# Eight buffers of split weights at eight byte offsets modulo 128 in a hybrid recurrent block in float32

## The chip, the cores and the metric

One Trainium2 chip, one of its cores. The metric is the time of one execution on the device in microseconds. The engines are named as in the profile: PE is TensorE's matmul, PEld its weight load (the load of the operand that stands still), DVE is VectorE, ACT ScalarE, POOL GpSimd, SP SyncE, whose queue issues nearly all transfers.

## The reference

One layer over 512 positions of width 1024, in float32: a mixer of two recurrent branches (HGRN2 and mLSTM, four heads of 128 each), a cross attention to 256 memory rows, and a feed-forward part with a causal convolution of three taps. Each ends in a residual and a layer norm:

```python
mix = hybrid_mixer(x, w_in[l], b_in[l], lower_bounds[l], hg_norm_w[l],
                   ml_conv_w[l], ml_conv_b[l], ml_norm_w[l], w_out[l])
x = layer_norm(ALPHA * x + mix, ln1_g[l], ln1_b[l])
ca = memory_cross_attention(x, mem, ca_wq[l], ca_wkv[l], ca_wo[l])
x = layer_norm(ALPHA * x + ca, ln2_g[l], ln2_b[l])
ff = conv_ffn(x, ffn_w_up[l], ffn_conv_w[l], ffn_conv_b[l], ffn_w_down[l])
x = layer_norm(ALPHA * x + ff, ln3_g[l], ln3_b[l])
```

The work is in the dense products with `w_in` (1024 x 4104), `w_out`, `ca_wq`, `ca_wkv`, `ca_wo` (1024 wide), `ffn_w_up` (1024 x 5632) and `ffn_w_down` (2816 x 1024).

## The kernel before

**Products in three terms.** Each operand of a dense product is held as a rounded high part (float32r) and a low part, the rest. `mm3` (line 155) issues three matmuls for one product: high by high (L156), high by low (L157), low by high (L158). The activations are split once where they are made (`split_evict`, line 244) into tiles such as `xTh` and `xTl`. The weights are split on the way: a transfer brings up to 8 KiB a partition into `raw` (three buffers), and `split` (line 119) makes two units of it. For each unit ACT copies 1024 elements a partition into a buffer `wh`, rounding them (L125), and DVE subtracts that from `raw` into a buffer `wl` (L126). There are four `wh` and four `wl` of 4096 bytes a partition, used in turn; a copy into one waits until the matmuls that read its earlier contents are done.

**Two kinds of stage.** In `slab` (line 160) the activations stand still in the array and 512 columns of weights stream past: for each unit of two k-blocks, over up to four blocks of 128 positions, high, low and high parts of the weights are streamed in turn. The slabs are four column ranges of `w_in` (HI by a loop written out at lines 278 to 303, HG, MV, MO), `w_out`, the values of the cross attention, `ca_wo` and `ffn_w_down`. In `col_tile` (line 200) the weights stand still, 128 columns at a time, and the activations stream: `w_in`'s other ranges, the keys (256 columns), `ca_wq` and `ffn_w_up` (halves of 256 columns at its beginning). In the profile's names `mm<-wh,xTh` is a matmul that streams `wh` while `xTh` stands still, and `mm<-x2h,wh` one that streams `x2h` past `wh`. One unit feeds 24 matmuls of 512 columns in either kind, fewer where there are only two blocks.

**The gate columns.** The 8 columns of `w_in` for the mLSTM gates take a turn of the four `wh` buffers by themselves (line 350): POOL clears the buffer, ACT and DVE write high and low parts into it, and the matmuls of L362 and L363 load it.

**Where tiles lie.** The pools follow one another within a partition: `const`, `wp` (`raw`, `wh`, `wl`, the gate columns), `xp` (ten activation tiles of 8 KiB), `sm` (small vectors), and then `q1` or `q2`. Paddings (`CONST_PAD`, `WP_PAD`, `SM_PAD`) make `raw`, `wh`, `wl` and every large activation tile begin at a multiple of 128 bytes; slices of them begin at further multiples of 512 bytes.

**Order.** The order of the opening (transposes of x and the HI product) is written out by hand; elsewhere each engine runs its instructions in the order of the program as it was scheduled. Nothing of that order is named in the change.

Of the kernel before, what the change touches and what calls it, by code (L numbers as in the profile page):

```python
# [10 lines left out]
F32R = mybir.dt.float32r  # L11
# [6 lines left out]
P = 128  # L18
# [3 lines left out]
KT = D // P  # L22
# [7 lines left out]
QSCALE = P ** -0.5  # L30
CSCALE = 256 ** -0.5
WARM = 7
CONST_PAD, WP_PAD, SM_PAD = 40, 64, 16
HQ, HF, HI, HG, MQ, MK, MV, MO, MI, MF = (0, 512, 1024, 1536, 2048, 2560, 3072, 3584, 4096, 4100)


# [1 line left out]
def hybrid_block_kernel(  # L38
# [31 lines left out]
    wp = ctx.enter_context(tc.tile_pool(name="wp", bufs=1))  # L70
# [26 lines left out]
    def f32(t):  # L97
        return t.bitcast(F32)
# [12 lines left out]
    def load_raw(src_list, shape):  # L111
# [4 lines left out]
            nc.sync.dma_start(dst, src)  # L116
        return rv

    def split(src, shape):
        h = wp.tile([P, 1024], F32R, name="wh", tag="wh", bufs=4)  # L120
        l = wp.tile([P, 1024], F32R, name="wl", tag="wl", bufs=4)
        a, c = shape
        hv = h.rearrange("p (a c) -> p a c", a=a)
        lv = l.rearrange("p (a c) -> p a c", a=a)
        A.copy(hv, src)  # L125
        V.tensor_sub(lv, src, f32(hv))  # L126
        return hv, lv

    def slab_units(w, c0, nk, raw=None):

        k, per = 0, (2 if raw is not None else 4)
        while k < nk:
            n = min(4, nk - k)
            if k or raw is None:
                raw = load_raw(
                    lambda rv, k=k, n=n: [(rv[:, j:min(j + per, n), :],
                                           w[(k + j) * P:(k + min(j + per, n)) * P, c0:c0 + 512]
                                           .rearrange("(k p) c -> p k c", p=P)) for j in range(0, n, per)],
                    (4, 512))
            for u in range(0, n, 2):  # L140
                h, l = split(raw[:, u:u + 2, :], (2, 512))
                yield k + u, 2, h, l
            k += n

    def col_units(w, c0, n):

        for j in range(0, n, 2):
            raw = load_raw(
                lambda rv, j=j: [(rv, w[:, c0 + j * P:c0 + (j + 2) * P]
                                  .rearrange("(k p) c -> p k c", p=P))], (8, 256))  # L150
            for i in range(2):
                h, l = split(raw[:, :, i * P:(i + 1) * P], (8, P))
                yield j + i, h, l
# [193 lines left out]

    wif = wp.tile([P, KT, 8], F32, name="wif")
    nc.sync.dma_start(wif, w_in0[:, MI:MI + 8].rearrange("(k p) c -> p k c", p=P))
    wifh = wp.tile([P, 1024], F32R, name="wh", tag="wh", bufs=4).rearrange("p (k c) -> p k c", k=KT)  # L350
    G.memset(f32(wifh), 0.0)
    for j in range(2):
        src = wif[:, :, 4 * j:4 * j + 4]
        o, o2 = slice(32 * j, 32 * j + 4), slice(64 + 32 * j, 68 + 32 * j)
# [183 lines left out]
    for hd in range(4):  # L538
        o = hgrn_head(hd)
# [36 lines left out]
    for j in range(4):  # L576
        ps = mm_bank()
        for i in range(2):
            for b in range(2):
                k = 2 * j + i  # L580
# [257 lines left out]
    def up_units(i):  # L838
        raw = load_raw(lambda rv: [(rv[:, :, j * P:(j + 1) * P],
                                    ffn_w_up[0][:, j * DFF + i * P:j * DFF + (i + 1) * P]  # L840
                                    .rearrange("(k p) c -> p k c", p=P)) for j in range(2)], (8, 256))
        return [split(raw[:, :, j * P:(j + 1) * P], (8, P)) for j in range(2)]
# [4 lines left out]
    for half in range(2):  # L847
        c0 = half * 256
        for i in range(early):
            for j in range(2):  # L850
                if (half, i, j) == (0, 1, 1):
                    x2_last()
                h, l = units[i][j]
# [31 lines left out]
def build(shapes):  # L885
    import concourse.bacc as _bacc

    nc = _bacc.Bacc("TRN2", target_bir_lowering=False, num_devices=1, dynamic_dma_scratch_size=1024)
    args = [nc.dram_tensor(f"in_{n}_dram", shapes[n], F32, kind="ExternalInput").ap() for n in _INS]
    args.append(nc.dram_tensor("out_0_dram", (1, S, D), F32, kind="ExternalOutput").ap())  # L890
    with tile.TileContext(nc) as tc:
        hybrid_block_kernel(tc, *args)
    return nc
# [9 lines left out]
```

## Time and profile before

| | |
|---|---|
| three runs | 828.69, 829.31, 829.79 us; median 829.31 |
| profiled execution | 829.24 us, of which the span is 827.5 |
| PE busy | 809.6 us (98%), 4051 matmuls |
| PEld busy | 682.2 us (82%), beside PE |
| DVE busy | 504.4 us (61%) |
| ACT busy | 323.1 us (39%) |
| POOL busy | 31.6 us (4%) |
| transfers | 87.88 MB, 106 GB/s over the span |

The span runs from the first to the last instruction. A matmul's recorded duration overlaps that of the next, so a busy PE does not tell how fast it goes: the distance from one start to the next does, and it is worked out from the rows of a timeline. "Idle before" is the time for which an engine did nothing ahead of an instruction, with what ended it.

### The profile page before, as it was taken

The numbers are of one execution on the slowest core, as the hardware profiler recorded it, in microseconds if no ns is written. First come the engines' busy times: TensorE is split into PE (matmuls) and PEld (weight loads), VectorE is DVE, ScalarE is ACT, GpSimd is POOL, SyncE is SP. The second block draws the span as 40 slices with busy tenths as digits, with TensorE's granted clock in tenths as the row PEclk, the third lists the DMA queues.
The fourth block names the chain that finished last, engine by engine and source line by source line (L and its number), as shares of the span: only waits on it lengthen the run. The fifth ranks groups of instructions, "written<-read, shape, count | busy, mean of one in ns | idle before, by whom it ended". The sixth has DMA issues, their size and how long they took to land.

```text
span 827.5 us, 10149 instructions
## 1 busy us (share of the span) xinstructions
PE 809.6 (98%) x4051; PEld 682.2 (82%) x4051; DVE 504.4 (61%) x863; ACT 323.1 (39%) x443; POOL 31.6 (4%) x52
## 2 busy tenths in 40 slices
PE   8979999999999999999999999999999999999996
PEld 7868877778779888889988988888888888888885
DVE  4374378888878289338638685566665666224237
ACT  4169653344235215226512364444444444221110
POOL 1000100010120000000001000000000000000001
PEclk9999999999999999999999999999999999999998
DMA  7845534034426613431311533333333322242102
GB/s 250 188 93 134 133 65 102 12 91 102 143 74 220 239 51 137 168 102 52 102 51 51 154 104 101 102 102 102 102 103 101 91 83 83 75 153 70 59 0 102
DMA packets 85156, 87.88 MB, mean 106 GB/s; under 512 B 3184, under 2 KB 64880, under 8 KB 85108
## 3 DMA queue, kind: packets, MB, share of 16 engines
q1 hardware_dynamic: 84524, 84.58, 34.4%
q10 hardware_dynamic: 584, 2.64, 0.8%
q8 instruction: 32, 0.52, 0.3%
q14 instruction: 16, 0.13, 0.0%
HBM read 85.10 MB, written 2.12 MB: 105 GB/s over the span
## 4 chain that ended last, share of the span: by engine, by line
PE 88%; DVE 5%; DMA 3%; POOL 1%; ACT 1%; issue 1%; SPq 0%; DVEq 0%; ACTq 0%; POOLq 0%
PE mm L156 27%; PE mm L157 27%; PE mm L158 27%; DMA raw<-in_w_in_dram 3%; PE mx L254 1%; PE mx L605 1%; PE mx L617 1%; POOL ss L451 1%; DMA xin<-in_x_dram 1%; PE mx L492 1%; PE mx L493 1%; PE mx L156 0%; PE mx L158 0%; PE mx L157 0%; PE mx L445 0%
## 5 line engine op out<-in xcount | busy, mean ns | idle before, releaser
L126 DVE TENSOR_TENSOR wl<-raw,wh 128x1024 fp32r<-128x1024 f32 x138 | 168.1, 1223 | 233.1 <-ACT wh L125 232.1
L125 ACT CAST wh<-raw 128x1024 fp32r<-128x1024 f32 x138 | 145.2, 1055 | 247.9 <-PE mm L158 135.1
L156 PE MATMUL mm<-x2h,wh 128*128 128x512 f32 (+1 forms) x384 | 142.8, 372 | 0.0
L157 PE MATMUL mm<-x2l,wh 128*128 128x512 f32 (+1 forms) x384 | 142.6, 371 | 0.0
L158 PE MATMUL mm<-x2h,wl 128*128 128x512 f32 (+1 forms) x384 | 142.6, 371 | 0.0
L158 PEld LDWEIGHTS mm<-x2h,wl 128*128 128x128 f32 x384 | 72.4, 188 | 12.6
L157 PEld LDWEIGHTS mm<-x2l,wh 128*128 128x128 f32 x384 | 72.4, 188 | 12.5
L156 PEld LDWEIGHTS mm<-x2h,wh 128*128 128x128 f32 x384 | 72.4, 188 | 12.3
L157 PE MATMUL mm<-wl,hTh 128*128 128x512 f32 (+1 forms) x198 | 72.4, 366 | 0.0
L156 PE MATMUL mm<-wh,hTh 128*128 128x512 f32 (+1 forms) x198 | 72.4, 366 | 0.0
L826 DVE SCALAR_TENSOR_TENSOR fc<-mm,cols,fc 128x511 f32<-128x511 f32 x88 | 65.7, 747 | 1.5
L158 PE MATMUL mm<-wh,hTl 128*128 128x512 f32 (+1 forms) x180 | 65.8, 365 | 0.0
L156 PE MATMUL mm<-wh,xTh 128*128 128x512 f32 x128 | 52.1, 407 | 0.0
L158 PE MATMUL mm<-wh,xTl 128*128 128x512 f32 x128 | 51.6, 403 | 0.0
L157 PE MATMUL mm<-wl,xTh 128*128 128x512 f32 x128 | 51.4, 401 | 0.0
L156 PE MATMUL mm<-xTh,wh 128*128 128x512 f32 x128 | 51.2, 400 | 0.0
L157 PE MATMUL mm<-xTl,wh 128*128 128x512 f32 x128 | 51.0, 399 | 0.0
L158 PE MATMUL mm<-xTh,wl 128*128 128x512 f32 x128 | 50.9, 397 | 0.0
L156 PEld LDWEIGHTS mm<-wh,hTh 128*128 128x128 f32 x198 | 37.4, 189 | 6.1
L157 PEld LDWEIGHTS mm<-wl,hTh 128*128 128x128 f32 x198 | 37.4, 189 | 6.1
L158 PEld LDWEIGHTS mm<-wh,hTl 128*128 128x128 f32 x180 | 33.9, 189 | 5.5
L835 ACT CAST hTh<-fc 128x512 fp32r<-128x512 f32 x22 | 13.7, 622 | 55.8 <-DVE fc L834 55.8
(274 smaller groups left out, 1401.3 us busy)
## 6 DMA issues: line engine op xcount, KB each, us to landing
raw<-in_ffn_w_up_dram SPq DMA_DIRECT2D x44, 512.0 KB, 4.3
raw<-in_w_in_dram SPq DMA_DIRECT2D x14, 1024.0 KB, 8.1
raw<-in_ffn_w_down_dram SPq DMA_DIRECT2D x10, 1024.0 KB, 5.0
raw<-in_ca_wkv_dram SPq DMA_DIRECT2D x8, 1024.0 KB
raw<-in_w_out_dram SPq DMA_DIRECT2D x4, 1024.0 KB, 10.1
raw<-in_ca_wq_dram SPq DMA_DIRECT2D x4, 1024.0 KB, 7.2
raw<-in_ca_wo_dram SPq DMA_DIRECT2D x4, 1024.0 KB
wt<-scr ACTq DMA_DIRECT2D x4, 640.0 KB
```

The lines of the kernel that those rows point to most:

```text
L125: A.copy(hv, src)
L126: V.tensor_sub(lv, src, f32(hv))
L156: T.matmul(ps, ah, bh, start=first, stop=False, skip_group_check=True)
L157: T.matmul(ps, ah, bl, start=False, stop=False, skip_group_check=True)
L158: T.matmul(ps, al, bh, start=False, stop=last, skip_group_check=True)
L254: T.transpose(ps[:, i * P:(i + 1) * P], src[:, k * P:(k + 1) * P], ident)
L451: G.tensor_tensor(out_, out_, neghalf[:, 0:n], op=OP.pow)
L492: T.matmul(at[:, s], ke[:, s], qe[:, s], start=True, stop=True, skip_group_check=True)
L493: T.matmul(at[0:CH, b * P + CH:(b + 1) * P], kxe[:, b, :], qbo[:, b, :], start=True, stop=True, skip_group_check=True)
L605: T.matmul(ps[:, 0:LEN[j]], kT_[:, j * P:(j + 1) * P], qT_[:, j * P:], start=True, stop=True)
L826: V.scalar_tensor_tensor(y[:, s:], ps[:, :S - s], col(FCW + (2 - s) * 44 + ft), y[:, s:], op0=OP.mult, op1=OP.add)
L835: A.copy(kslice(hTh, i), g)
```

## The change

Each of the eight buffers becomes a tile of its own, 1056 elements long instead of 1024, and the 1024 that are used begin at an offset within it: 16, 32, 48 and 8 bytes for the four high parts, 80, 96, 112 and 64 bytes for the four low parts. The tiles themselves are a multiple of 128 bytes long and begin at one, so these are the offsets modulo 128 to the activations. `split_tiles` hands out a high and a low part by turns. The gate columns take a pair and use its high part. `WP_PAD` goes from 64 to 32 elements.

```diff
-CONST_PAD, WP_PAD, SM_PAD = 40, 64, 16
+CONST_PAD, WP_PAD, SM_PAD = 40, 32, 16
+
+PHASES = {"wh": (16, 32, 48, 8), "wl": (80, 96, 112, 64)}
...
+    turn = [0]
+
+    def split_tiles():
+
+        i = turn[0] % 4
+        turn[0] += 1
+        out = []
+        for t in ("wh", "wl"):
+            o = PHASES[t][i] // 4
+            out.append(wp.tile([P, 1056], F32R, name=t, tag=f"{t}{i}")[:, o:o + 1024])
+        return out
+
     def split(src, shape):
-        h = wp.tile([P, 1024], F32R, name="wh", tag="wh", bufs=4)
-        l = wp.tile([P, 1024], F32R, name="wl", tag="wl", bufs=4)
+        h, l = split_tiles()
...
-    wifh = wp.tile([P, 1024], F32R, name="wh", tag="wh", bufs=4).rearrange("p (k c) -> p k c", k=KT)
+    wifh = split_tiles()[0].rearrange("p (k c) -> p k c", k=KT)
```

## Rows read from the trace of the kernel before

**Rows 1.** Stretches: length; busy us (instructions) of PE, PEld, DVE, ACT, POOL; clock; transfers.

```profile
30.00:70.00 40.00, 35.65 (x155) 29.06 (x154) 24.90 (x50) 23.44 (x27) 0.00 (x0) 0.96 0.48 118
...
480.00:760.00 280.00, 280.00 (x1245) 232.23 (x1244) 156.54 (x188) 110.14 (x138) 0.00 (x0) 1.00 0.33 100
```

**Rows 2.** Waits of PE, whole span: us in total, times, longest.

```profile
PE mx L404 <- ACT ae L399: 4.3, 1, 4.3
PE mx L445 <- DVE y L534: 2.4, 3, 1.1
PE mx L254 <- DMA xin<-in_x_dram: 1.6, 1, 1.6
...
PE mx L617 <- DVE den L627: 0.3, 1, 0.3
```

**Rows 3.** Timeline of PE in the FFN, weights standing: start, us, instruction.

```profile
545.73 0.39 PE L156 MATMUL mm<-x2h,wh 128*128 128x512 f32 x1
...
551.85 0.39 PE L156 MATMUL mm<-x2h,wh 128*128 128x512 f32 x1
```

**Rows 4.** Timeline of PE in the first slab, weights streaming.

```profile
20.17 0.39 PE L158 MATMUL mm<-wh,xTl 128*128 128x512 f32 x1
...
35.13 0.39 PE L158 MATMUL mm<-wh,xTl 128*128 128x512 f32 x1
```

**Rows 5.** Timeline of PE at the end of the last slab, 256 columns.

```profile
816.87 0.28 PE L156 MATMUL mm<-wh,hTh 128*128 128x256 f32 x1
...
819.99 0.28 PE L158 MATMUL mm<-wh,hTh 128*128 128x256 f32 x1
```

**Rows 6.** The whole span as a stretch, instructions with a `wh`, then with a `wl`.

```profile
0.00:827.50 827.50, 666.07 (x2268) 416.48 (x2268) 168.45 (x140) 145.58 (x140) 0.95 (x1) 1.00 0.36 106
...
0.00:827.50 827.50, 423.13 (x1126) 213.23 (x1126) 168.13 (x138) 1.00 0.36 106
```

**Rows 7.** A stretch at the lower clock, and PE's timeline in it.

```profile
61.90:65.10 3.20, 3.20 (x8) 2.52 (x9) 1.28 (x3) 3.19 (x5) 0.00 (x0) 0.50 0.00 0
...
62.41 0.63 PE L157 MATMUL mm<-xTl,wh 128*128 128x512 f32 x1
...
64.54 0.63 PE L156 MATMUL mm<-xTh,wh 128*128 128x512 f32 x1
```

**Rows 8.** Timeline of PE where 512 columns follow 256 in the FFN.

```profile
481.79 0.40 PE L156 MATMUL mm<-x2h,wh 128*128 128x512 f32 x1
...
482.95 0.39 PE L158 MATMUL mm<-x2h,wl 128*128 128x512 f32 x1
...
483.85 0.39 PE L156 MATMUL mm<-x2h,wh 128*128 128x512 f32 x1
```

**Rows 9.** Groups of PEld by form: count, busy us, mean ns, idle before.

```profile
L156 PEld LDWEIGHTS mm<-x2h,wh 128*128 128x128 f32 x384 | 72.4, 188 | 12.3
...
L493 PEld LDWEIGHTS mx<-xo 128*64 128x64 f32 x32 | 3.1, 134 | 2.1 <-issue 0.2
```

**Rows 10.** Groups of DVE and of ACT by form, same columns.

```profile
L126 DVE TENSOR_TENSOR wl<-raw,wh 128x1024 fp32r<-128x1024 f32 x138 | 168.1, 1223 | 233.1 <-ACT wh L125 232.1 <-PE mm L581 0.8
...
L826 DVE SCALAR_TENSOR_TENSOR fc<-mm,cols,fc 128x511 f32<-128x511 f32 x44 | 32.8, 744 | 0.0
...
L704 DVE SCALAR_TENSOR_TENSOR xres<-xres,lnrs,lnb 128x512 f32<-128x512 f32 x24 | 16.9, 746 | 0.0
...
L125 ACT CAST wh<-raw 128x1024 fp32r<-128x1024 f32 x138 | 145.2, 1055 | 247.9 <-PE mm L158 135.1 <-PE mm L157 79.3 <-DMA raw<-in_w_in_dram 13.4
```

**Rows 11.** Waits of ACT, then of DVE, between 500 and 760 us.

```profile
ACT wh L125 <- PE mm L158: 40.0, 10, 4.4
...
DVE wl L126 <- ACT wh L125: 104.0, 48, 4.3
```

**Rows 12.** The chain that ended last, in order of time: start, us, what.

```profile
18.76 20.91 DMA raw<-in_w_in_dram
39.77 1.06 ACT wh L125
```

## The prediction

> **What bounds the kernel now.** I read the stretches of the span first, then what ended TensorE's idle time, then TensorE's rows one by one. The stretches [rows 1] show TensorE busy in nearly every microsecond: 280.00 of 280.00 us between 480 and 760 us, and short of full only for moments, such as 4.35 us between 30 and 70 us. The waits [rows 2] show six groups in which TensorE idled: 4.3 us for ScalarE, 2.4 us for VectorE, 1.6 us for a transfer, and three smaller ones, the last of 0.3 us. None waits for a split weight buffer. So the time is the number of matmuls times the distance from one start to the next. A busy TensorE does not say how good that distance is, so I worked it out from starts: in the FFN 27 matmuls from 545.73 to 551.85 us, more than the 24 that one pair of buffers feeds, take 6.12 us, 226.7 ns each [rows 3]. In a slab, where the weights stream and the activations stand still, 66 matmuls from 20.17 to 35.13 us take 14.96 us, again 226.7 ns [rows 4]. Matmuls of 256 columns start every 3.12 us / 26 = 120.0 ns [rows 5]. The 256 columns between the two sizes cost 106.7 ns, 0.417 ns a column (the 2.4 GHz level, granted 1.00 in those stretches). So 512 columns stream in 213.3 ns, and each matmul of either size carries 13.3 ns on top.
>
> The split buffers are operands of 2268 + 1126 = 3394 matmuls [rows 6]. 3394 x 13.3 ns = 45.2 us of the span is this surplus. The change can pay, or cost, almost only there.
>
> **What is known of the surplus.** At the 1.2 GHz level (granted 0.50 from 61.90 to 65.10 us) five starts from 62.41 to 64.54 us are 426 ns apart: 512 columns at 0.833 ns are 426.7, and no surplus is left [rows 7]. It is no fixed cost in ns of a matmul; it shows where the stream runs at its full rate. It is also 32 columns of 4 bytes at 0.417 ns, so just as long as 128 bytes of one partition's stream, the very period in which the change places its buffers. But 128 weights of 4 bytes being loaded beside it could give 32 of something too. And it is not quite constant: where matmuls of 512 columns follow those of 256, the first five take 482.95 - 481.79 = 1.16 us instead of 1.133, and from then on the distance is 226.7 again (0.90 us for the next four) [rows 8]. Two streams seem to fall into step there, in 27 ns.
>
> **The change, part by part.** No instruction, transfer or wait is added or taken away in the loops; the same eight slots are used in turn. What moves:
>
> The offsets. Before, pool sizes make every large tile begin at a multiple of 128 bytes, weights and activations alike, and slices step by 512 bytes or more. After, the eight slots begin 8, 16, 32, 48 (high parts) and 64, 80, 96, 112 bytes (low parts) past that. In 1458 matmuls (the slabs: 384 + 192 + 192 + 96 + 594 by the loops) the streaming operand is shifted, in the other 1936 the one being loaded. What that does to 226.7 ns no row shows, since all of the trace has offset zero. The bounds are the rows at either end: all of the surplus gone (-45.2 us), or a second one on each of the 1458 shifted streams (+19.4 us). The reason to stand near zero between them: a load moves at half the stream's rate. A load of 128 columns takes 188 ns, one of 64 columns 134 ns [rows 9], so 54 / 64 = 0.84 ns a column against 0.417. While a load reads its 512 bytes the stream passes 1024, so the two slide past each other through four whole turns of 128 bytes. Wherever they begin, they meet at each relative place equally often; an offset moves the moment of a meeting, not the number. I take 0 us.
>
> The Trainium skill speaks against any effect: its page "TensorE: Matmul & The Clock Gate", section "Step-by-step: what each phase is for", gives TensorE two independent read ports, and says that loading the next weights takes no read bandwidth from the running matmul; by that rule the sum changes by nothing. The same page, section "Wait — 56ns, not 53.3ns?", has a warm matmul take its columns plus about 2.5 ns, where this trace shows 13.3, so the page leaves 10.8 ns of the surplus without a cause; if the offsets took just that away, an estimate by the page would be 3394 x 10.8 ns = 36.7 us less.
>
> The writers. ScalarE's rounding copy (1055 ns) and VectorE's subtraction (1223 ns) now write, and the second also reads, shifted buffers, 138 times each [rows 10]. On VectorE a start inside a buffer costs nothing: an FFN tap begins 4 bytes in and takes 744 ns, an aligned step with as many operands 746 [rows 10]. For ScalarE no row shows a shifted write; I bound it by 0 and a tenth of a copy. Both are covered: between 500 and 760 us the copies waited 40.0 us for the matmuls of L158 alone to free their buffer, and VectorE 104.0 us for the copies [rows 11]. Without that cover the tenth would be 138 x 0.1 us = 14 us. I take 0.
>
> The slots. The tile with the gate columns of w_in used to take a turn of the high parts alone, now of both. So the next three low parts reuse a buffer three splits old instead of four. Those subtractions follow copies from 39.77 us on, and the slab that read these buffers was over at 35.13 us [rows 4, 12]: 0 us.
>
> The pools. The padding shrinks by 128 bytes and the eight buffers grow by 8 x 128, so everything after them moves by 896 bytes, 7 x 128, and the raw weights by -128: still offset zero. Where transfers land has changed with that. They count where the chain of waits stands on them, 20.91 us in the opening up to the copy at 39.77 us [rows 12]. No row shows such a landing; I take 0 and, as an estimate, a tenth of that stretch, 2 us either way, as its bounds.
>
> **Sum.** 829.24 (the profiled execution: a span of 827.5 and 1.7 around it, 0.07 below the median 829.31) + 0 = 829.2 us. 0.2% is about what a measurement of this kernel can tell from no change, so "same" means 827.6 to 830.9.
>
> **Rivals.**
>
> Half a turn saved (faster). The surplus is a wait for the stream to come round to the same place in its 128 bytes. For it: its size of 32 columns at 512 and at 256 columns, its absence at half the clock, and the falling into step [rows 3, 5, 7, 8]. Then in a slab, where high, low and high parts stream in turn and low lies half a turn (64 bytes, in one slot 56) from high, two of three waits shrink from 13.3 to 6.7 ns: 4.4 ns x 1458 = 6.5 us, 822.7. If the loaded operand counts likewise, 4.4 x 3394 = 15.1 us, 814.1. Against it: a wait for one's turn should also show at half the clock, if only smaller.
>
> The surplus gone (faster). Load and stream clash because both begin at offset zero, and any other offset ends it: -45.2 us, 784.0. Against it: the 2:1 sliding worked out above.
>
> Out of step (slower). What settles in five matmuls at offset zero must settle anew whenever a slot with another offset comes up, or cannot settle at all. At 27 ns for each of 138 units it is 3.7 us, 832.9; if it never settles, 5.3 ns (27 / 5) on 3394 matmuls is 18.0 us, 847.2. It decides from the point where a unit's first matmuls don't start 226.7 ns apart. For it: the settled state is only known with all operands at zero. Against it: the first matmuls of a new unit in the FFN now cost nothing extra [rows 3].
>
> One block more (slower). If the stream is fetched in blocks of 128 bytes, a shifted slab operand touches 17 instead of 16: 13.3 ns x 1458 = 19.4 us, 848.6. For it: the surplus is as long as one block. Against it: no row.
>
> Nothing done at all would be the forecast itself: the distance is set inside TensorE and offsets don't enter.
>
> **Chances.** Forecast 0.38; half a turn 0.25; surplus gone 0.08; out of step 0.17; one block more 0.08; something in the opening from the moved landings or the clock's low stretch 0.04 (0.03 of it slower). So faster 0.25 + 0.08 + 0.01 = 0.34, same 0.38, slower 0.17 + 0.08 + 0.03 = 0.28. For 8 in 10 I go from 815 to 843: that leaves out the vanished surplus, the block and the far ends of the half turn and of being out of step, together some 0.19. The forecast's own range is 827.6 to 830.9; the chances lie on both sides of it because the one quantity that matters has no row at another offset.
>
> **What the profile after would show.** The distance between starts in the FFN (weights loaded) and in the slabs (weights streamed), taken apart: both 226.7 ns if the forecast holds; 226.7 and a mean near 222 for the half turn; 213 to 216 in both for a vanished surplus; 240 in slabs alone for the block; runs like those of [rows 8] at each new unit, or throughout, for out of step. If high and low parts differ in a slab, the turn matters. Copies and subtractions should stay at 1055 and 1223 ns, and TensorE's waits those of [rows 2]. The prediction is wrong if the distance moves by over 0.5 ns in either kind of stage, since 0.5 x 3394 is already 1.7 us.

## The result, and the profile after

The changed kernel takes 840.34 us (median of 4 runs, 839.1 to 840.75) where the kernel before takes 829.49 (828.69 to 829.79): a ratio of 1.013, 95% interval 1.0112 to 1.0147. It is slower by 1.3%. The forecast was no change, put at 827.6 to 830.9; the time lies outside that and inside 815 to 843, the range for 8 in 10, which was that wide for the rivals' sake. The profiled execution took 840.44 us with a span of 838.7, 11.2 us more than before, and that difference is what the readings below account for.

The stretches of [rows 1], read again in the kernel after (length; busy us and instructions of PE, PEld, DVE, ACT, POOL; clock; transfers):

```profile
30.00:70.00 40.00, 35.18 (x148) 28.21 (x147) 24.44 (x50) 22.54 (x27) 0.00 (x0) 0.91 0.50 118
480.00:760.00 280.00, 280.00 (x1238) 228.71 (x1237) 154.85 (x185) 112.08 (x140) 0.00 (x0) 1.00 0.33 96
```

TensorE is again busy in every microsecond between 480 and 760 us, at a granted clock of 1.00, and yet gets through 1238 matmuls instead of 1245. The waits of PE over the whole span (us in total, times, longest) are those of [rows 2], longer by 0.5 us at L417 (L404 before) and 0.9 at L267 (L254 before):

```profile
PE mx L417 <- ACT ae L412: 4.8, 1, 4.8
PE mx L267 <- DMA xin<-in_x_dram: 2.5, 1, 2.5
PE mx L458 <- DVE y L547: 2.4, 3, 1.1
...
PE mx L630 <- DVE den L640: 0.3, 1, 0.3
```

The groups by line show the writers of the shifted buffers (L138 and L139, which were L125 and L126 in [rows 10]), the last figures being their idle time and what ended it:

```profile
L139 DVE TENSOR_TENSOR wl<-raw,wh 128x1024 fp32r<-128x1024 f32 x138 | 167.9, 1221 | 241.7 <-ACT wh L138 240.4 <-PE mm L594 0.9
...
L138 ACT CAST wh<-raw 128x1024 fp32r<-128x1024 f32 x138 | 144.4, 1049 | 258.2 <-PE mm L171 150.3 <-PE mm L170 85.3 <-DMA raw<-in_w_in_dram 13.6
```

A copy takes 1049 ns (1055 before) and a subtraction 1221 (1223): a shifted write costs nothing. The two longer waits lie in the opening, and where it ends shows what they come to. The chain that ended last, in order of time, before and then after:

```profile
61.45 0.43 PE mx L404 x4
```

```profile
40.12 1.06 ACT wh L138
...
61.79 0.64 PE mx L417 x4
```

The matmuls at which the longest wait ends start 0.3 us later than before. The other 10.9 us are lost behind them, where no wait has grown, so they must be in the distances between starts. TensorE's timeline in the FFN, weights standing (start, us, instruction), first over a long stretch and then from one matmul to the next:

```profile
495.41 0.40 PE L169 MATMUL mm<-x2h,wh 128*128 128x512 f32 x1
...
547.47 0.39 PE L169 MATMUL mm<-x2h,wh 128*128 128x512 f32 x1
547.69 0.39 PE L170 MATMUL mm<-x2l,wh 128*128 128x512 f32 x1
547.92 0.40 PE L171 MATMUL mm<-x2h,wl 128*128 128x512 f32 x1
548.16 0.40 PE L169 MATMUL mm<-x2h,wh 128*128 128x512 f32 x1
548.39 0.39 PE L170 MATMUL mm<-x2l,wh 128*128 128x512 f32 x1
548.62 0.40 PE L171 MATMUL mm<-x2h,wl 128*128 128x512 f32 x1
548.86 0.40 PE L169 MATMUL mm<-x2h,wh 128*128 128x512 f32 x1
...
695.39 0.40 PE L169 MATMUL mm<-x2h,wh 128*128 128x512 f32 x1
```

From the first to the last of these rows there are 864 matmuls: 199.98 us / 864 = 231.5 ns, where [rows 3] have 226.7. Single distances are 0.22, 0.23, 0.24, 0.23, 0.23 and 0.24 us; they never settle. Taken by the pair of buffers that a unit uses, the mean is 231.0, 231.2, 231.0 and 232.6 ns, and from the second of ten rounds on it comes out the same in each. So it is not noise: each arrangement has its own rhythm.

The slabs, weights streaming, by the same view, 30 matmuls apart (first slab), and the 256-column products at the end of the last slab, 27 matmuls apart:

```profile
25.75 0.39 PE L169 MATMUL mm<-wh,xTh 128*128 128x512 f32 x1
...
32.71 0.39 PE L169 MATMUL mm<-wh,xTh 128*128 128x512 f32 x1
...
825.97 0.28 PE L169 MATMUL mm<-wh,hTh 128*128 128x256 f32 x1
...
829.15 0.28 PE L169 MATMUL mm<-wh,hTh 128*128 128x256 f32 x1
```

The first two give 6.96 / 30 = 232.0 ns against 226.7 in [rows 4]. The last two give 3.18 / 27 = 117.8 ns against 120.0 in [rows 5]: with 256 columns the change saves.

Summed over all starts of the two profiled executions: the 512-column products with weights standing go from 226.85 to 231.51 ns a matmul (1520 of them, +7.1 us), those of the slabs from 227.32 to 231.65 (1277, +5.5 us). Those held up by a wait or by the lower clock are left out of these means (86 before, 81 after). All 512-column products together, with these: 671.91 to 683.80 us, +11.9. The 256-column ones give back 0.9 us, everything else adds 0.2. 11.9 - 0.9 + 0.2 = 11.2 us, the whole difference of the spans. (7.1 and 5.5 are 12.6; the matmuls left out regain 0.7 on balance, since six of the opening that started 402 to 427 ns apart before start 226 to 275 apart after.)

### The profile page after: what moved, and what is told of

Read it like the earlier page. It is cut to its first block, busy times and chain, and to the rows that moved or that the text cites. A ratio compares the mean times of both kernels' runs of the same rounds, so it can differ in the third digit from the quotient of the medians.

```text
span 838.7 us, 10149 instructions
## 1 busy us (share of the span) xinstructions
PE 819.6 (98%) x4051; PEld 681.4 (81%) x4051; DVE 504.3 (60%) x863; ACT 322.4 (38%) x443; POOL 31.6 (4%) x52
## 4 chain that ended last, share of the span: by engine, by line
PE 89%; DVE 4%; DMA 3%; POOL 1%; ACT 1%; issue 1%; SPq 0%; DVEq 0%; ACTq 0%; POOLq 0%
PE mm L169 27%; PE mm L170 27%; PE mm L171 27%; DMA raw<-in_w_in_dram 2%; PE mx L267 1%; PE mx L618 1%; PE mx L630 1%; POOL ss L464 1%; DMA xin<-in_x_dram 1%; PE mx L505 1%; PE mx L506 0%; PE mx L169 0%; PE mx L171 0%; PE mx L170 0%; PE mx L458 0%
## 5 line engine op out<-in xcount | busy, mean ns | idle before, releaser
L139 DVE TENSOR_TENSOR wl<-raw,wh 128x1024 fp32r<-128x1024 f32 x138 | 167.9, 1221 | 241.7 <-ACT wh L138 240.4
L138 ACT CAST wh<-raw 128x1024 fp32r<-128x1024 f32 x138 | 144.4, 1049 | 258.2 <-PE mm L171 150.3
L169 PE MATMUL mm<-x2h,wh 128*128 128x512 f32 (+1 forms) x384 | 144.9, 377 | 0.0
L171 PE MATMUL mm<-x2h,wl 128*128 128x512 f32 (+1 forms) x384 | 143.5, 374 | 0.0
L171 PEld LDWEIGHTS mm<-x2h,wl 128*128 128x128 f32 x384 | 72.3, 188 | 14.3
L171 PE MATMUL mm<-wh,hTl 128*128 128x512 f32 (+1 forms) x180 | 66.2, 368 | 0.0
L171 PE MATMUL mm<-wh,xTl 128*128 128x512 f32 x128 | 51.5, 402 | 0.0
L171 PE MATMUL mm<-xTh,wl 128*128 128x512 f32 x128 | 51.5, 402 | 0.0
L171 PEld LDWEIGHTS mm<-wh,hTl 128*128 128x128 f32 x180 | 33.9, 188 | 6.1
```

Of the source, the lines that this page charges most:

```text
L169: T.matmul(ps, ah, bh, start=first, stop=False, skip_group_check=True)
L171: T.matmul(ps, al, bh, start=False, stop=last, skip_group_check=True)
```

## The experiments

**Are the offsets the cause?** Everything of the change stays (eight tiles of 1056 elements, the paddings), only the offsets become zero.

```diff
-PHASES = {"wh": (16, 32, 48, 8), "wl": (80, 96, 112, 64)}
+PHASES = {"wh": (0, 0, 0, 0), "wl": (0, 0, 0, 0)}
```

> The changed kernel with all eight offsets at zero; tiles of 1056 elements, their slots, the gate columns' pair and the padding stay as changed. Relative (the distance between matmul starts hangs on where the streamed and the loaded operand lie to each other modulo 128): 226.7 ns in both kinds of stage, 829.3 us. Absolute (it hangs on where each operand begins within 128 bytes): the same, 829.3. Layout (the slots, the longer tiles or the 896 bytes by which the other pools moved cost the time): 840, with starts some 231 ns apart.

Measured: 838.1 us, ratio 1.0109 (1.0094 to 1.0124). The offsets are gone and most of the loss is still there. Of the 2.6 us by which its profiled span is shorter than the changed kernel's (836.1 against 838.7), 1.7 lie in the opening (L417 starts at 60.07 us, not 61.79). Its timeline in the FFN, nine matmuls:

```profile
547.93 0.39 PE L169 MATMUL mm<-x2h,wh 128*128 128x512 f32 x1
548.16 0.40 PE L170 MATMUL mm<-x2l,wh 128*128 128x512 f32 x1
...
550.01 0.39 PE L169 MATMUL mm<-x2h,wh 128*128 128x512 f32 x1
```

2.08 / 9 = 231.1 ns. So either the layout of the tiles does it without any offset, or one of the other edits. The next three kernels were written before this was known:

```diff
 # e_abs64: offsets zero, and all that follows the constants 64 bytes further
-CONST_PAD, WP_PAD, SM_PAD = 40, 32, 16
+CONST_PAD, WP_PAD, SM_PAD = 56, 32, 16
...
 # e_cols: offsets where weights stand; e_slabs: kind == "slab" in its place
-            o = PHASES[t][i] // 4
+            o = PHASES[t][i] // 4 if kind == "col" else 0
...
-                h, l = split(raw[:, u:u + 2, :], (2, 512))
+                h, l = split(raw[:, u:u + 2, :], (2, 512), "slab")
```

> All offsets at zero, and everything behind the constants moved by 64 bytes: raw weights, split weights and all activations begin at 64 modulo 128, so the operands of each product lie to each other as before the change. Relative: 226.7 ns, 829.3 us. Absolute: at least as slow as the changed kernel, 840 or more, as every operand now begins within a block.

Measured: 837.83 us, 1.0101 (1.0084 to 1.0118), the same 231.1 ns in the FFN. Moving weights and activations together by 64 bytes changes nothing; a stream fetched in blocks of 128 bytes ("one block more") would have paid for this in every product.

> The offsets are used only where weights stand still and activations stream (col_units, the FFN's up product, the gate columns); in slabs the buffers begin at zero. Relative: the standing weights' 1520 matmuls of 512 columns keep their 231.5 ns (+7.1 us against 226.9), the slabs go back to 226.7: 829.3 + 7.1 - 0.8 (the products of 256 columns came out 2 ns quicker each) = 835.6. Absolute with only the streamed operand counting: 829.3. Absolute with only the loaded one counting: 835.6 as well.

> The other half: offsets only in slabs, where weights stream. Relative: the slabs' matmuls keep their 231.7 ns, the rest goes back to 226.7: 829.3 + 1275 x 4.4 ns = 834.9 us. Absolute with only the loaded operand counting: 829.3. With the run before, the two parts add up to the change (6.3 + 5.6 = 11.9 against 10.9 us measured) if the stages don't depend on each other.

Measured: 840.09 us (1.0133, 1.0118 to 1.0148) and 839.53 us (1.0127, 1.0112 to 1.0142). Both expectations missed, since they started from 829 without offsets and the kernel without offsets already stands at 838. What can be read from them is that the offsets add little on top: with weights standing 231.51 ns with offsets (e_cols) and 231.12 without (e_slabs), in the slabs 231.75 with (e_slabs) and 232.04 without (e_cols). In e_zero the slabs without offsets have 230.34. The difference lies in the last slab: 229.0 ns in e_zero and 231.7 in e_cols, by the mean of its 462 undisturbed matmuls, with the same buffers at the same places. Only the stages with standing weights ahead of it had other offsets. So the rhythm depends on what ran before, too.

**Which edit beside the offsets?** Three are left: the padding, the eight slots with their new order, and the tile length of 1056 elements, 4224 bytes. The pool sizes show what the last one does. Before, every buffer is 4096 bytes long. After, the low part of a pair lies 4224 bytes behind its high part, which is 16 x 256 + 128, so without any offset the high parts lie a multiple of 256 bytes from the activations and the low parts half of that further. Four kernels take these apart:

```diff
 # f_zero_pad64: tiles of 1056, offsets zero, the padding as before
-CONST_PAD, WP_PAD, SM_PAD = 40, 32, 16
+CONST_PAD, WP_PAD, SM_PAD = 40, 64, 16
...
 # f_zero_1024: the same, with tiles of the old length
-            out.append(wp.tile([P, 1056], F32R, name=t, tag=f"{t}{i}")[:, o:o + 1024])
+            out.append(wp.tile([P, 1024], F32R, name=t, tag=f"{t}{i}")[:, o:o + 1024])
...
 # f_offsets_1152: the offsets of the change, the padding as before, tiles of 4608 bytes (18 x 256)
+            out.append(wp.tile([P, 1152], F32R, name=t, tag=f"{t}{i}")[:, o:o + 1024])
...
 # f_before_pad32: the kernel before with the new padding
-CONST_PAD, WP_PAD, SM_PAD = 40, 64, 16
+CONST_PAD, WP_PAD, SM_PAD = 40, 32, 16
```

> All eight offsets at zero, tiles of 1056 elements as changed, but the padding back to 64 elements: activations begin at 0 modulo 512 again (with the padding of 32 they begin at 384). High and low part of a pair still lie 4224 bytes apart, 128 modulo 512. Activations' place (the changed kernel is slower because activations no longer begin at a multiple of 512 bytes): 226.7 ns between matmul starts, 829. Pair distance (it is slower because high and low part no longer lie a multiple of 512 apart, 128 bytes being the 32 columns by which three matmuls grew from 680 to 693 ns): 231.1 ns, 838.

> The kernel before with the padding of 32 elements alone: weights and activations all move by -128 bytes, activations to 384 modulo 512; the buffers lie as before, pairs a multiple of 512 apart. Activations' place: 231 ns, 838. Pair distance: 226.7 ns, 829.

> Eight tiles with slots as changed, all offsets at zero, but each 1024 elements long and the padding at 64: high and low part 4096 bytes apart, activations where they were before the change. What stays of the change is the eight slots, the order of the buffers (high, low, high, low) and the gate columns' pair. Activations' place and pair distance: 226.7 ns, 829. Slots or order of the buffers: 838.

> The changed kernel with its eight offsets, but tiles of 1152 elements (4608 bytes, a multiple of 512) and the padding at 64: activations at 0 modulo 512, pairs 64 bytes apart modulo 512 (56 in one slot). This is what the change names, by itself. Activations' place alone: 829. Pair distance: 64 bytes are 16 columns, 6.7 ns on three matmuls, 2.2 ns x 3394 = 7.5 us, 837; if any distance but zero costs a whole step, 840. Relative to the activations (offset against offset): 829 plus the 2.2 us by which the changed kernel is above the one with all offsets at zero, 831.

| kernel | us | ratio, 95% interval | 512 columns in the FFN, ns |
|---|---|---|---|
| f_zero_pad64 | 837.43 | 1.0096, 1.0079 to 1.0112 | 231.1 |
| f_before_pad32 | 828.91 | 0.9994, 0.9984 to 1.0005 | 226.7 |
| f_zero_1024 | 828.54 | 0.9996, 0.9987 to 1.0005 | 226.7 |
| f_offsets_1152 | 839.92 | 1.0131, 1.0113 to 1.0148 | 230.7 to 233.2 by pair |

The FFN of f_zero_pad64, 18 matmuls, and of f_zero_1024, 21:

```profile
547.79 0.39 PE L169 MATMUL mm<-x2h,wh 128*128 128x512 f32 x1
...
551.95 0.39 PE L169 MATMUL mm<-x2h,wh 128*128 128x512 f32 x1
```

```profile
546.67 0.39 PE L169 MATMUL mm<-x2h,wh 128*128 128x512 f32 x1
...
551.43 0.39 PE L169 MATMUL mm<-x2h,wh 128*128 128x512 f32 x1
```

4.16 / 18 = 231.1 and 4.76 / 21 = 226.7 ns: eight tags, their order of turns and the gate columns' pair cost nothing, and neither does the padding. Between f_zero_pad64 and f_zero_1024 only the tile length differs, and it is worth 837.43 - 828.54 = 8.9 us (behind the opening of the profiled executions, from the start of L417 on, 776.2 against 766.1 us). The offsets alone, with the length put right, are worth 11 us. So the change contains two causes; each is enough by itself, and together they cost no more than the larger one. That fits a settled rhythm that is either kept or lost, and not a price for each byte.

**Modulo what?** By the change's own terms, modulo 128, a tile length of 4224 is as good as 4096. If the period is 256 bytes, an offset of 128 in all eight buffers must cost as much as the odd ones, and one of 256 nothing. Both kernels have tiles of 1152 elements and the padding as before; the sweep that the first expectation names is the study of trains further down, which ran ahead of them:

```diff
 # u_128; u_256 has 256 in all eight places
-PHASES = {"wh": (16, 32, 48, 8), "wl": (80, 96, 112, 64)}
+PHASES = {"wh": (128, 128, 128, 128), "wl": (128, 128, 128, 128)}
```

> The changed kernel with tiles of 1152 elements and the padding at 64 (pairs a multiple of 512 apart, activations at 0 modulo 512) and one offset for all eight buffers: 128 bytes. By the change's own measure this is offset zero modulo 128. Period 128 (what counts is the place modulo 128): 226.7 ns, 829. Period 256 with load against stream (the sweep: 233.3 ns with weights standing, 232.3 with weights streaming): 829.2 + 1520 x 6.5 + 1275 x 5 ns = 845, less 1 us in the products of 256 columns. Pair distance (only a distance between high and low part costs, a common offset doesn't): 829.

> The same with all eight offsets at 256 bytes. Period 256: 226.7 ns, 829. Period 512 or longer: 840 or more.

Measured: u_128 841.98 us, 1.0152 (1.0135 to 1.0169), the slowest of all, some 2.5 us less than its expectation; u_256 828.53 us, 0.9992 (0.9983 to 1.0001). The FFN of u_128:

```profile
546.88 0.40 PE L169 MATMUL mm<-x2h,wh 128*128 128x512 f32 x1
547.12 0.39 PE L170 MATMUL mm<-x2l,wh 128*128 128x512 f32 x1
547.35 0.40 PE L171 MATMUL mm<-x2h,wl 128*128 128x512 f32 x1
547.59 0.39 PE L169 MATMUL mm<-x2h,wh 128*128 128x512 f32 x1
...
551.08 0.40 PE L169 MATMUL mm<-x2h,wh 128*128 128x512 f32 x1
```

and of u_256:

```profile
548.10 0.39 PE L169 MATMUL mm<-x2h,wh 128*128 128x512 f32 x1
...
550.14 0.39 PE L169 MATMUL mm<-x2h,wh 128*128 128x512 f32 x1
```

4.20 / 18 = 233.3 ns and 2.04 / 9 = 226.7 ns. The missing 2.5 us are mostly the opening: u_128 starts L417 at 59.49 us, 2.0 earlier than L404 before, and loses 14.8 us behind it. In the profiled executions of all these kernels the opening ends between 59.5 and 61.8 us, in no order with the offsets, so one or two us between two kernels need not be distances.

Here all eight buffers lie alike, high and low, in every slot, and none moves against another, so the distance between high and low part, a rival of several expectations, is not needed for the loss. It is not the weights' absolute place either: f_before_pad32 moves weights and activations together by 128 bytes and keeps 226.7 ns. It is the place of weights against activations that counts, modulo 256 bytes.

**The distance by itself.** Trains of 48 matmuls on TensorE alone, with no writer and no transfer beside them, each on a line of its own in the text. In "col" trains the weights stand (as in the FFN), in "slb" trains they stream, and "one" repeats a single pair of operands; `rel` is the weights' offset against the activations, `dl` that of the low weights, `dx` that of the low activations, in bytes (in the code all are counted in elements of 4 bytes, `k` is the k-block, and `WL` and `XL - 128` are where the low parts begin, multiples of 256 bytes). Both studies of trains leave the layer's work out and ran once.

```diff
...
+    def col(i, rel, dl, dx, n=512):
+        k, r = (i // 3) % 8, i % 3
+        s = rel + k * 128 + (WL + dl if r == 2 else 0)
+        m = k * 512 + (XL - 128 + dx if r == 1 else 0)
+        return W[:, s:s + 128], X[:, m:m + n]
...
```

> Leaves the whole computation out: 54 trains of 48 matmuls (after 60 to warm up) on two float32r tiles, W (weights) and X (activations), three matmuls a step as in the kernel (high-high, high-low, low-high), each train with other byte offsets: of W to X, of W's low part to its high part, of X's low part to its high part. Distances between starts are read from each train's second half. Pair distance (what costs is that consecutive loads, or consecutive streams, don't lie at the same place modulo 512): with pairs at 0, any common offset of W to X gives 226.7 ns; a pair distance of 128 bytes gives 231.1 ns, one of 64 bytes 230 to 232, also where it is the streamed activations' pair. Relative to the activations: a common offset of W to X of 16 to 128 bytes gives 231 and more, pair distances matter only through it. Clash of lines: pitches differ between offsets of 4, 8 and of 16 bytes, as a line of 16 bytes is split by the first two.

Each row of TensorE's timeline is one train here, and the difference of two starts is 48 distances. In the first group `rel` is 128, 192, 256, 384 and 0 from L131 to L135; in the second `dx` is 64, 128 and 256 from L146 to L148; in the third, with 256 columns, all is zero in L171, `rel` 64 in L172 and `dl` 64 in L173:

```profile
133.27 11.36 PE L131 MATMUL mm<-X,W 128*128 128x512 f32 x48
144.47 11.16 PE L132 MATMUL mm<-X,W 128*128 128x512 f32 x48
155.46 11.06 PE L133 MATMUL mm<-X,W 128*128 128x512 f32 x48
166.36 11.32 PE L134 MATMUL mm<-X,W 128*128 128x512 f32 x48
177.52 11.05 PE L135 MATMUL mm<-X,W 128*128 128x512 f32 x48
188.40 11.25 PE L136 MATMUL mm<-X,W 128*128 128x512 f32 x48
...
299.13 11.30 PE L146 MATMUL mm<-X,W 128*128 128x512 f32 x48
310.27 11.34 PE L147 MATMUL mm<-X,W 128*128 128x512 f32 x48
321.45 11.06 PE L148 MATMUL mm<-X,W 128*128 128x512 f32 x48
332.35 11.24 PE L149 MATMUL mm<-X,W 128*128 128x512 f32 x48
...
575.45 5.91 PE L171 MATMUL mm<-X,W 128*128 128x256 f32 x48
581.20 5.82 PE L172 MATMUL mm<-X,W 128*128 128x256 f32 x48
586.85 5.82 PE L173 MATMUL mm<-X,W 128*128 128x256 f32 x48
592.51 5.88 PE L174 MATMUL mm<-X,W 128*128 128x256 f32 x48
```

`rel` 128 takes 11.20 / 48 = 233.3 ns, 192 takes 229.0, 256 (with a moment of settling) 227.1, 384 again 232.5, and 0 takes 226.7. `dx` 128 takes 232.9, 256 227.1. With 256 columns the order is the other way round: 119.8 at zero, 117.7 and 117.9 off it. Taken over the last 24 matmuls of each train, 226.67 ns stand where all offsets are multiples of 256, and in one train more (a single pair at `rel` 16, below); every other train with 512 columns has 228.9 to 234.4. So the rival of the pair distance falls: a common offset costs by itself. No train has an offset of 4 bytes, as the clash of lines would have wanted; `rel` 8 and 16 (230.7 and 233.3 ns) lie no further apart than multiples of 16 do among themselves (228.9 at 192, 234.4 at 96).

In the FFN, and with `rel` 128, the kernels follow the trains: `dl` 128 alone (as in e_zero) gives 231.12 with weights standing, where e_zero has 231.15; `rel` 128 gives 233.33 and 232.29 ("col" and "slb"), where u_128 has 232.96 and 232.41. The slabs of e_zero do so only in part: `dl` 128 gives 228.92 in "slb", and the last slab has 228.97, the others 231.12.

**Is there a better place, and is the settled rhythm a state that is remembered?** 99 further trains, 68 of them with 512 columns at places off zero, nearly all drawn at random, and at the beginning one offset of 16 bytes behind different forerunners.

> Leaves the whole computation out: 99 trains of 48 matmuls as in the sweep, offsets in steps of 16 bytes below 256: 44 random ones of W to X, of W's pair and of X's pair with W standing, 24 with W streaming, 18 of 256 columns; ahead of them 12 trains that ask whether a settled state outlives an offset (the same two operands again and again, offsets 0, 16, 128, 0, 32 bytes in turn). Period 256: 226.7 ns only where every offset is zero, 228 to 235 elsewhere, nothing below 226.7 with 512 columns, 117 to 120 with 256. If some offset is better than none, a train of 512 columns falls below 226. If the state before decides, offset 16 is 226.7 behind offset 0 and 231 to 234 behind offset 128.

The 68 trains run from 228.9 to 235.6 ns with a mean of 231.5, but for one (`rel` 144, `dl` 240, `dx` 160) that has 226.67, and none is below 226.67. There is no better place among them. The first trains of this timeline are all zero (L122), "one" at `rel` 16 (L123), at 128 (L124), at 16 (L125), all zero again (L126), "one" at 32 (L127), and all zero (L128):

```profile
42.52 11.05 PE L123 MATMUL mm<-X,W 128*128 128x512 f32 x48
53.41 11.32 PE L124 MATMUL mm<-X,W 128*128 128x512 f32 x48
64.57 11.36 PE L125 MATMUL mm<-X,W 128*128 128x512 f32 x48
75.77 11.05 PE L126 MATMUL mm<-X,W 128*128 128x512 f32 x48
86.66 11.36 PE L127 MATMUL mm<-X,W 128*128 128x512 f32 x48
97.85 11.05 PE L128 MATMUL mm<-X,W 128*128 128x512 f32 x48
```

The same train at 16 bytes takes 10.89 / 48 = 226.9 ns behind the settled one and 11.20 / 48 = 233.3 behind the one at 128. A settled rhythm outlives an offset of 16 bytes, but once lost is not found again there; at zero it comes back. An offset of 32 bytes breaks it at once (11.19 / 48 = 233.1 ns, right behind a settled train).

## Why the prediction was wrong

**What held.** The bound is TensorE, stage by stage, and its measure is the distance between starts: 10.9 of the 11.2 us lie behind the opening, in distances, with no wait grown. The buffers are operands of 3394 matmuls, and that is where the change acts. The writers (1049 and 1221 ns), the slots and their order (f_zero_1024) and the common shift of all pools (f_before_pad32) cost 0, as put down; where transfers land was given 2 us either way, and the copy in the opening that started at 39.77 us [rows 12] starts at 40.12. The list of what the profile would show names the cases rightly: 5 ns in both kinds of stage, throughout, is "out of step".

**The step that failed** is the end of the paragraph on the offsets: a load at half the stream's rate slides past it through four turns of 128 bytes, so "an offset moves the moment of a meeting, not the number", hence 0 us. It should have read +11.2 us (231.51 ns in place of 226.85 with weights standing, 231.65 in place of 227.32 in the slabs). The argument takes the surplus as a sum of chance meetings whose mean an offset can't change. The trains show that there is no such mean: at zero the two operands run in one fixed rhythm (227, 227, 226 ns), at other places in others (229 and 238 by turns at `rel` 128), and the mean of the rhythm depends on the place. [Rows 8] had shown this in small: five matmuls at 232 ns until the distance falls to 226.7. I priced that row under "out of step" and left it out of the sum.

**The second failed step** is in the paragraph on the pools, and before it in "all of the trace has offset zero". I took 128 bytes as the period because the surplus is as long as 32 columns of 4 bytes, and the diff speaks of 128 too; with that the tile length of 4224 bytes is "still offset zero". The period is 256 (u_128 and u_256), and the length alone costs 8.9 us (f_zero_pad64 against f_zero_1024). No row of before could tell 128 from 256, since the kernel before keeps to 256 in all of these products; the working should have given the length its own bounds, as it did for the offsets.

**The rivals.** Out of step is what happened. Its larger price, 847.2, was 18.0 us for 3394 matmuls at 5.3 ns. Measured are 4.7 ns (weights standing) and 4.3 ns (slabs) on 2797 of 512 columns; the 497 undisturbed ones of 256 columns, which the price counted as losers, gain 1 to 2 ns each. Half a turn saved (822.7 or 814.1) falls: the high and low parts half of 128 bytes apart in the slabs give 231 to 232 ns, not 222. The surplus gone (784.0) falls: of the 130 trains with 512 columns in both studies none is below 226.67. One block more (848.6, slabs alone) falls with e_abs64 and with the loss where weights stand.

The Trainium skill, page "TensorE: Matmul & The Clock Gate", section "Step-by-step: what each phase is for", has loads and streams on two read ports of their own, so that a load takes nothing from the running matmul. By that rule u_128 and u_256 would take the same time. They differ by 841.98 - 828.53 = 13.4 us, with nothing changed but where the weights lie; here the measurement decides against that reading of it.

**What stays open.** Why the period is 256 bytes, what keeps or loses the rhythm, why one train off zero (`rel` 144, `dl` 240, `dx` 160) settles all the same, and why products of 256 columns gain off zero. That the settled rhythm outlives a small offset was seen only in trains; in the kernels only the last slab of e_cols against e_zero shows a rhythm that depends on what ran before. Offsets in the 256-column stages alone might keep the 0.9 us that the change gives back there; that was not tried, being 0.1% of the time.

## What to carry to other kernels

Where products have 512 columns, keep all float32r operands of TensorE that meet, weights and activations, high and low parts, at one place modulo 256 bytes, and count the lengths of the tiles between them, not only the offsets: a tile of 4224 bytes did nearly as much harm (8.9 us) as eight odd offsets (11). When a change moves buffers, look at single distances between starts first (here 226, 227, 227 ns in step, and 226 to 239 in changing order out of step): the busy share of TensorE stays at 100% either way. And test a change of several parts by undoing each part, its padding and lengths too, since undoing the part that gave it its name brought 840.3 us down to 838.1 only.

## What the runs showed of the hardware

- With float32r operands and 512 columns, a matmul starts every 226.67 ns if weights and activations lie at the same place modulo 256 bytes, and every 228.9 to 235.6 ns (mean 231.5 over the 68 trains) otherwise, with one exception in 68 and the trains of the state below. Moving all operands together by 64 or 128 bytes has no influence (e_abs64, f_before_pad32).
- With 256 columns it is the reverse: 120.0 ns at the same place, 117.4 to 119.0 at all others tried in trains but one (120.0 at `rel` 160).
- The settled rhythm behaves like a state: an offset of 16 bytes keeps it (226.9 ns) and doesn't restore it (233.3 ns); one of 32 bytes loses it (233.1 ns).
